# Second norm's rows on VectorE, expert weights split behind the last residual, the second expert's gather asked for later, and two tiles weighed by diagonal matmuls, in a two-layer trunk

## The chip, the cores and the metric

The kernel runs on one core of a Trainium2 chip. The metric is the device time of one execution in microseconds (us). Three runs of the kernel before gave a median of 2047.85 us (2045.67 to 2050.42). About 0.2% of that, 4 us, is what a measurement of this kernel can tell from no change.

Engine names in the rows: PE is TensorE, DVE is VectorE, ACT is ScalarE, POOL is GpSimd, SP is SyncE (here it only issues DMAs).

## What is computed

Two layers over 256 latent tokens and 256 context tokens of width 1024, all in float32. Each layer mixes the tokens (three branches, an output projection and a gated residual), then runs a mixture of 16 experts, of which each token takes two. What the change touches is the second half of a layer and the way into the next one:

```
mix = merge_branches(gate_l, y_hy, y_gdn, y_mla, lp['w_out'])
x = x + (gt1 * mix).astype(x.dtype)
h2 = rms_norm(x, lp['norm2_g']) * (1.0 + sc2) + sh2
x = x + (gt2 * moe_ffn(h2, ...)).astype(x.dtype)
...
# moe_ffn: two experts of 16 per token, with weights that sum to 1
for e in range(N_EXPERTS):
    he = jax.nn.silu(h @ lp['moe_w1'][e]) * (h @ lp['moe_w3'][e])
    out = out + gate[:, e:e + 1] * (he @ lp['moe_w2'][e])
```

The first layer updates all 512 tokens, the second the 256 latent ones alone. A final RMSNorm follows.

## The kernel before

**Tiles.** Tokens lie in tiles of 128 rows, four in layer 0 (two latent, two context), two in layer 1. Buffers are pages of 128x512 floats, taken from a pool; most rows of the trace call them `pg`, and PSUM banks `bank`. One helper (line 207) records every operation, so that rows of the trace tell operations apart by tiles and shapes and not by lines.

**Order.** The order of the instructions on each engine is fixed when the program is built: work is written as items (weights, their preparation, matmuls, what comes behind them) and as streams, which are Python generators with a priority. A planner keeps a modelled clock for each engine and lets a stream go on where the engine that it needs would be idle. Each engine then runs its queue strictly in order.

**Weights in layer 0.** A 128x1024 block of weights is split into a high part (ACT, a CAST to fp32r) and a low part (DVE, a subtraction, `TENSOR_TENSOR pg<-pg,pg 128x1024 fp32r`). `mm3` then makes each product out of three fp32r matmuls. `prep_ahead` (line 520) splits blocks some items ahead of their use; the flag `quiet` holds it still. Layer 1's experts (`moe_sets`) use plain f32 matmuls and split nothing.

**The second norm and the route.** `wout_items` (line 1783) makes the output projection in two groups of two tiles, tile 1 of a group four steps behind tile 0. Behind a tile's last matmul stands its residual on DVE (two pairs of 128x512 operations), and then its stream `ffn_in` (line 1863): squares on ACT, transposes on PE, a Newton chain of twelve small DVE operations for the factor `r` (tiles `t_rf0` to `t_rf3`), the row h2 = (x r) A2 + B2, its DMA to DRAM (`h2d`), and the router's scores. In layer 0 the row is one DVE `TENSOR_SCALAR` and two POOL `TENSOR_TENSOR`s, in layer 1 it goes without A2 and B2. When all scores are there, the stream `route` (line 1930) picks two experts for each token (tiles `t_rsc`, `t_rsel`, `t_rpr`, `t_rgs`, `t_rmx`, `t_rt`, `t_rmk`, `t_rtop`, `t_rix`, `t_rxf`, `t_ro`, `t_rA`), gathers expert 0's rows by a matmul of h2 with a one-hot matrix, and for experts 1 to 3 asks POOL for gathers by index from `h2d` (`t_gi`). `route` does the first three tiles' selection ahead of the last one's. At its gathers it clears `quiet` (line 2047).

**Experts.** An expert of layer 0 (`moe_items`) has two halves j, each with four steps q of six matmuls, and then its second projection; 12 blocks of weights in all. At step (0, 0) of expert e it starts the stream `expert_in` of expert e+1: eight PE transposes of the gathered rows and their split. Layer 1 goes by 12 sets (`moe_sets`) of four experts' quarters, and starts the next set's rows at the same place.

**Between the layers.** The experts' outputs lie in DRAM (`yd`). `load_y` loads both of a tile's outputs, tiles 0 to 3 in order. `combine` (line 2387) weighs each tile's pair (ACT y0 gw0, then DVE y1 gw1 + y0), multiplies by the gate (POOL for three tiles, DVE for the last), adds to the residual (DVE) and squares (ACT). Then a Newton chain for all four tiles, the first norm of layer 1, transposes on PE, and layer 1's input projection. From the last matmul of layer 0's experts until those transposes PE has nothing to do.

## Time and profile before

| | |
|---|---|
| median of three runs | 2047.85 us |
| the profiled execution's own time | 2048.27 us, of which its span is 2045.2 |
| PE busy | 1842.3 us (90%) |
| DVE busy | 1281.2 us (63%) |
| ACT busy | 870.9 us (43%) |
| POOL busy | 312.1 us (15%) |
| layer 0, output projection to first expert | 785 to 885 us of the span |
| layer 0, experts | 885 to 1157 us |
| between the layers | 1157 to 1190 us |
| layer 1, route and first set | 1740 to 1773 us |
| layer 1, experts | to 2034 us |

PE is busy nine tenths of the time; what the kernel could save elsewhere shows only where PE waits. A timeline row gives the start, the duration, the engine, the helper's line, the operation with output and inputs, the count of like operations that were put together, and in brackets how long the engine stood idle before the row and what it waited for.

### The profile page before, as it was taken

Reading aid. Unit: us, or ns where it says so; the run is one execution under the profiler, and the core shown is the slowest. Engines: PE = TensorE matmul, PEld = TensorE weight load, DVE = VectorE, ACT = ScalarE, POOL = GpSimd, SP = SyncE. Lnnn points to the kernel's source line nnn. Section 1 sums busy time; section 2 is a strip of 40 time slices with the busy share of each in tenths; the row PEclk is TensorE's granted clock in tenths of the full one; section 3 lists DMA queues with packets and bytes.
Section 4 is the critical chain, followed back from the end, with each engine's and each line's share of the span. In section 5 each row is a group of like instructions: output and inputs, shape, how many; then the busy total and the mean of one; then the engine's idle time right before and its main releaser. Section 6 shows DMA issues by size and latency. Waiting matters only on the chain. (4 is left out here: it accounts for less than half of the span.)

```text
span 2045.2 us, 32512 instructions
## 1 busy us (share of the span) xinstructions
PE 1842.3 (90%) x12356; PEld 1358.6 (66%) x12357; DVE 1281.2 (63%) x2721; ACT 870.9 (43%) x1518; POOL 312.1 (15%) x323
## 2 busy tenths in 40 slices
PE   4899998999999989699999668998989968799997
PEld 1776786777778777578888546797867966333332
DVE  2667665755675669789999676768668665211113
ACT  3442423444433533278888544343554533111111
POOL 2212112000033104301110112121011211011000
PEclk9999998999999988799999889998989989899999
DMA  9816202602263255689999293822415428899991
GB/s 330 270 60 215 81 19 55 167 21 73 83 206 84 81 207 195 237 306 381 379 382 380 101 335 136 249 60 58 124 32 165 133 96 308 310 314 391 393 390 72
DMA packets 308207, 402.78 MB, mean 197 GB/s; under 512 B 56504, under 2 KB 198334, under 8 KB 308040
## 3 DMA queue, kind: packets, MB, share of 16 engines
q1 hardware_dynamic: 283480, 358.29, 52.6%
q0 software_dynamic: 14112, 30.94, 4.4%
q10 hardware_dynamic: 10448, 11.37, 1.7%
q8 instruction: 99, 1.62, 0.3%
q14 instruction: 68, 0.56, 0.1%
HBM read 391.94 MB, written 24.25 MB: 203 GB/s over the span
## 5 line engine op out<-in xcount | busy, mean ns | idle before, releaser
L207 PE MATMUL bank<-pg,pg 128*128 128x512 f32 (+7 forms) x10694 | 1649.4, 390 | 42.6 <-DVE pg L207 20.0
L207 PEld LDWEIGHTS bank<-pg,pg 128*128 128x128 f32 (+5 forms) x10694 | 1199.5, 166 | 439.9 <-issue 203.8
L207 DVE TENSOR_TENSOR pg<-pg,pg 128x1024 fp32r<-128x1024 f32 (+10 forms) x684 | 598.9, 909 | 156.1 <-ACT pg L207 149.1
L207 ACT CAST pg<-pg 128x1024 fp32r<-128x1024 f32 (+2 forms) x456 | 424.6, 967 | 191.9 <-DVE pg L207 133.2
L207 ACT COPY pg<-bank 64x256 f32<-64x256 f32 (+4 forms) x398 | 162.6, 441 | 282.2 <-PE bank L207 258.8
L207 PE MATMUL bank<-cst,pg 128*128 128x128 f32 (+3 forms) x935 | 149.0, 297 | 121.9 <-DVE pg L207 76.4
L207 PEld LDWEIGHTS bank<-cst,pg 128*128 128x128 f32 (+1 forms) x935 | 122.4, 165 | 169.8 <-issue 55.9
L207 POOL TENSOR_TENSOR pg<-pg,pg 128x512 f32<-128x512 f32 (+3 forms) x65 | 105.8, 1631 | 396.7 <-DVE pg L207 165.7
L207 ACT ACTIVATE pg<-bank 128x512 f32<-128x512 f32 (+1 forms) x116 | 61.2, 535 | 168.3 <-PE bank L207 160.2
L207 ACT ACTIVATE pg<-pg 128x512 f32<-128x512 f32 (+4 forms) x77 | 52.7, 692 | 146.5 <-DVE pg L207 113.5
L207 DVE SCALAR_TENSOR_TENSOR pg<-bank,vec,pg 128x510 f32<-128x510 f32 (+3 forms) x112 | 73.5, 657 | 57.9 <-ACT pg L207 55.9
L207 DVE SCALAR_TENSOR_TENSOR pg<-pg,bank 128x512 f32<-128x512 f32 (+1 forms) x92 | 54.4, 600 | 83.6 <-ACT pg L207 67.5
L207 POOL DMA_INDIRECT yd<-pg,t_vi x26 | 27.1, 1043 | 422.0 <-ACT pg L207 236.7
L207 DVE TENSOR_TENSOR pg<-pg,bank 128x512 f32<-128x512 f32 (+1 forms) x48 | 29.7, 618 | 87.1 <-PE bank L207 78.7
L207 DVE TENSOR_TENSOR pg<-bank,pg 128x512 fp32r<-128x512 f32 (+4 forms) x120 | 69.1, 596 | 22.4 <-ACT pg L207 7.6
L207 ACT CAST pg<-bank 128x512 fp32r<-128x512 f32 (+1 forms) x72 | 35.6, 517 | 102.0 <-PE bank L207 82.5
L207 POOL TENSOR_TENSOR pg<-pg 128x512 f32<-128x512 f32 (+1 forms) x14 | 17.2, 1236 | 401.0 <-ACT pg L207 350.9
L207 ACT ACTIVATE pg<-bank,vec 128x512 f32<-128x512 f32 (+3 forms) x64 | 41.4, 646 | 63.4 <-PE bank L207 58.8
L207 ACT ACTIVATE pg<-bank,t_amx,t_asq 128x512 f32<-128x512 f32 (+1 forms) x48 | 33.9, 707 | 74.9 <-DVE t_amx L207 74.9
L207 PE MATMUL bank<-pg,sc 128*32 128x512 f32 x384 | 54.1, 634 | 0.7 <-DMA pg<-in_w_ada_dram 0.7
L207 DVE COPY pg<-bank 128x512 f32<-128x512 f32 x10 | 6.9, 691 | 69.1 <-PE bank L207 62.2
L207 DVE TENSOR_REDUCE pg<-pg 128x128 f32<-128x1024 f32 (+15 forms) x128 | 43.0, 336 | 4.4
(268 smaller groups left out, 804.7 us busy)
## 6 DMA issues: line engine op xcount, KB each, us to landing
pg<-in_moe_w_dram SPq DMA_DIRECT2D x384, 512.0 KB
pg<-in_w_in_dram SPq DMA_DIRECT2D x120, 512.0 KB
pg<-in_w_ada_dram SPq DMA_DIRECT2D x96, 512.0 KB
pg<-in_w_out_dram SPq DMA_DIRECT2D x24, 512.0 KB
pg<-gcd POOLq DMA_DIRECT2D x16, 256.0 KB, 4.0
pg<-in_hy_out_dram SPq DMA_DIRECT2D x8, 512.0 KB
pg<-in_mla_out_dram SPq DMA_DIRECT2D x8, 512.0 KB
...
```

Of the source, the lines that this page charges most:

```text
L207: return f(*a, **k)
```

## The change

1. **Second norm, layer 0.** The row h2 leaves `ffn_in` and becomes a stream of its own, `row_out`, started behind the score. It is two DVE operations now, (x r) A2 by `SCALAR_TENSOR_TENSOR` and + B2 by `TENSOR_TENSOR`; POOL keeps the DMA. `route` waits for a tile's `row` ahead of the one-hot matmul and of the index part.
2. **Splits.** `quiet` is set from step 8 of the last group of the output projection on, and no longer at the last residual. Of expert 0's blocks one is split ahead of the route now, before it were four.
3. **Gather.** The rows of expert 1 (layer 0) and of set 1 (layer 1) are asked for at step (1, 0) of the first expert or set, so that their transposes stand behind its first half; later ones as before.
4. **Combine.** Tiles 0 and 2 run on ACT and DVE alone. For tiles 1 and 3, `diagonals` makes diagonal matrices of the weights (four 128x128 DVE operations, ahead of the outputs' last scatter), and PE adds up both products in PSUM (eight f32 matmuls 128x512); gate and residual then go in halves of 512 columns. `load_y` loads tiles in the order 0, 2, 1, 3. POOL has no part left.

The core of the diff:

```diff
@@ wout_items
+                if last and k > 7:
+                    self.quiet = True
...
-                    self.quiet = t == tiles - 1
@@ ffn_in
-        if l < L - 1:
-            A2, B2 = self.mod2[i]
-            v.tensor_scalar(h.f(), x.f(), r, None, op0=OP.mult)
-            g_.tensor_tensor(h.f(), h.f(), A2.f(), op=OP.mult)
-            g_.tensor_tensor(h.f(), h.f(), B2.f(), op=OP.add)
...
+        if l < L - 1:
+            self.start(f"row{t}", self.row_out(l, t, x, r), 2)
+
+    def row_out(self, l, t, x, r):
+        v = self.nc.vector
+        A2, B2 = self.mod2[t // 2]
+        h = self.h2[t]
+        yield
+        v.scalar_tensor_tensor(h.f(), x.f(), r, A2.f(), op0=OP.mult, op1=OP.mult)
+        v.tensor_tensor(h.f(), h.f(), B2.f(), op=OP.add)
...
+        self.nc.gpsimd.dma_start(out=self.h2d[l][128 * t:128 * t + 128], in_=h.f())
@@ route
+            for t in range(a, z):
+                yield f"row{t}"
...
+        for t in range(k):
+            yield f"row{t}"
@@ moe_items
-                if j == 0 and q == 0 and e + 1 < NE:
+                if (j, q) == ((0, 0) if e else (1, 0)) and e + 1 < NE:
@@ moe_sets
-                if j == 0 and q == 0 and n + 1 < NSET:
+                if (j, q) == ((0, 0) if n else (1, 0)) and n + 1 < NSET:
@@ load_y
-        for t in range(tiles):
+        for t in (0, 2, 1, 3):
@@ diagonals
+        self.dg = {t: self.M.get() for t in DIAG}
+        for t in DIAG:
+            for i in range(2):
+                self.nc.vector.tensor_scalar(self.dg[t].f(128, 128 * i), self.c("ident"), self.gw[i][:, t:t + 1], None, op0=OP.mult)
@@ combine
+        for t in DIAG:
+            for hf in range(2):
+                b = bank[t, hf] = self.bank()
+                for i in range(2):
+                    nc.tensor.matmul(b, self.dg[t].f(128, 128 * i), ys[t, i].f(512, 512 * hf), start=i == 0, stop=i == 1)
...
+            if t in DIAG:
+                for hf in range(2):
+                    o = 512 * hf
+                    v.tensor_tensor(y0.f(512, o), bank[t, hf], g.f(512, o), op=OP.mult)
...
+                    v.tensor_tensor(x.f(512, o), x.f(512, o), y0.f(512, o), op=OP.add)
+                    nc.scalar.activation(y1.f(512, o), x.f(512, o), AF.Square, accum_out=s8[:, 2 * t + hf:2 * t + hf + 1])
```

**DVE, layer 0, ahead of the last residual.** Tile 2's row (`pg_611`), its score, the first three tiles' selection up to `t_rgs`, then the residual of tile 3, which is the first `SCALAR_TENSOR_TENSOR` from a bank to a 128x512 page. Before:

```order
L207 TENSOR_SCALAR pg_611_6418<-pg_550_6020,t_rf2b 128x1024
L207 TENSOR_TENSOR pg_616_6463<-pg_560_6056,pg_615_6462 128x1024
L207 SCALAR_TENSOR_TENSOR score<-bank_65,t_rf2b,t_cB 128x16
L207 TENSOR_SCALAR t_rsc<-t_rsc 128x48
L207 TENSOR_TENSOR t_rsel<-t_rsc,rb 128x48
L207 TENSOR_TENSOR t_rpr<-t_rsel 128x12x3
L207 TENSOR_TENSOR t_rpr<-t_rsel 128x12x2
L207 TENSOR_TENSOR t_rpr<-t_rsel 128x12
L207 TENSOR_REDUCE t_rgs<-t_rpr 128x12
L207 TENSOR_TENSOR pg_620_6485<-pg_563_6074,pg_619_6484 128x1024
L207 TENSOR_TENSOR pg_624_6499<-pg_574_6132,pg_623_6498 128x1024
L207 SCALAR_TENSOR_TENSOR pg_627_6512<-bank_63,pg_553_6026 128x512
```

Now:

```order
L207 TENSOR_REDUCE t_rgs<-t_rpr 128x12
L207 SCALAR_TENSOR_TENSOR pg_611_6416<-pg_550_6020,t_rf2b,pg_557_6036 128x1024
L207 TENSOR_TENSOR pg_611_6416<-pg_611_6416,pg_558_6038 128x1024
L207 TENSOR_REDUCE t_rmx<-t_rgs 128x3
L207 TENSOR_TENSOR t_rt_6208<-t_rgs,t_rmx 128x12
L207 TENSOR_TENSOR t_rt_6208<-t_rt_6208,cst_72 128x12
L207 TENSOR_REDUCE t_rmx<-t_rt_6208 128x3
L207 TENSOR_TENSOR t_rgm<-t_rt_6208,t_rmx 128x12
L207 SCALAR_TENSOR_TENSOR pg_624_6508<-bank_63,pg_553_6026 128x512
L207 TENSOR_TENSOR pg_551_6022<-pg_551_6022,pg_624_6508 128x512
L207 SCALAR_TENSOR_TENSOR pg_624_6508<-bank_66,pg_553_6026 128x512
L207 TENSOR_TENSOR pg_551_6022<-pg_551_6022,pg_624_6508 128x512
```

The splits of blocks 560, 563 and 574 are gone from this place; tile 2's row (two operations) and five small ones stand there.

**PE, layer 0, expert 0.** The end of step (0, 0) and the transposes of expert 1's gathered rows (`cst<-` is the identity). Before:

```order
L207 MATMUL bank_66<-pg_608_6407,pg_636_6674 128x512
L207 MATMUL bank_66<-pg_607_6406,pg_637_6675 128x512
L207 MATMUL bank_69<-cst_71,pg_629_6518 128x128 x4
L207 MATMUL bank_68<-cst_71,pg_629_6518 128x128 x4
L207 MATMUL bank_66<-pg_615_6462,pg_636_6674 128x512
L207 MATMUL bank_66<-pg_616_6463,pg_636_6674 128x512
```

Now, at the end of step (1, 0):

```order
L207 MATMUL bank_69<-pg_647_6741,pg_633_6664 128x512
L207 MATMUL bank_69<-pg_646_6740,pg_634_6665 128x512
L207 MATMUL bank_68<-cst_71,pg_626_6514 128x128 x4
L207 MATMUL bank_70<-cst_71,pg_626_6514 128x128 x4
L207 MATMUL bank_69<-pg_648_6744,pg_633_6664 128x512
L207 MATMUL bank_69<-pg_649_6745,pg_633_6664 128x512
```

Four steps more, 24 matmuls, stand ahead of the transposes. On DVE, ten splits stand between the last `t_gw` and the first of expert 0's results where seven stood, and the rows' split stands behind the seventh, where it stood ahead of all; from expert 2 on, the kinds of operation come in the same order in both.

**DVE, between the layers.** `combine` from tile 0's residual on; `bank` is now an input. Before:

```order
L207 TENSOR_TENSOR pg_548_6016<-pg_548_6016,pg_1332_9823 128x1024
L207 SCALAR_TENSOR_TENSOR pg_1336_9831<-pg_1337_9833,t_gw,pg_1336_9831 128x1024
L207 TENSOR_TENSOR pg_549_6018<-pg_549_6018,pg_1334_9827 128x1024
L207 SCALAR_TENSOR_TENSOR pg_1338_9835<-pg_1339_9837,t_gw,pg_1338_9835 128x1024
L207 TENSOR_TENSOR pg_1338_9835<-pg_1338_9835,pg_632_6525 128x1024
L207 TENSOR_TENSOR pg_550_6020<-pg_550_6020,pg_1336_9831 128x1024
L207 TENSOR_TENSOR pg_551_6022<-pg_551_6022,pg_1338_9835 128x1024
L207 TENSOR_SCALAR t_css<-t_css 128x4
```

Now:

```order
L207 TENSOR_TENSOR pg_548_6016<-pg_548_6016,pg_1333_9824 128x1024
L207 SCALAR_TENSOR_TENSOR pg_1335_9828<-pg_1336_9830,t_gw,pg_1335_9828 128x1024
L207 TENSOR_TENSOR pg_1335_9828<-pg_1335_9828,pg_629_6521 128x1024
L207 TENSOR_TENSOR pg_550_6020<-pg_550_6020,pg_1335_9828 128x1024
L207 TENSOR_TENSOR pg_1337_9832<-bank_67,pg_628_6519 128x512
L207 TENSOR_TENSOR pg_549_6018<-pg_549_6018,pg_1337_9832 128x512
L207 TENSOR_TENSOR pg_1337_9832<-bank_70,pg_628_6519 128x512
L207 TENSOR_TENSOR pg_549_6018<-pg_549_6018,pg_1337_9832 128x512
L207 TENSOR_TENSOR pg_1339_9836<-bank_68,pg_629_6521 128x512
L207 TENSOR_TENSOR pg_551_6022<-pg_551_6022,pg_1339_9836 128x512
L207 TENSOR_TENSOR pg_1339_9836<-bank_69,pg_629_6521 128x512
L207 TENSOR_TENSOR pg_551_6022<-pg_551_6022,pg_1339_9836 128x512
```

Tile 2's residual moved ahead of tile 1's, and the last two tiles' work is in halves that wait for PE.

## Rows read from the trace of the kernel before

**Rows 1.** Windows: bounds, us, busy by engine, PEclk, DMA share, GB/s:

```profile
900.00:950.00 50.00, 50.00 (x235) 41.13 (x234) 47.30 (x48) 43.35 (x54) 7.11 (x6) 1.00 1.01 381
1190.00:1195.00 5.00, 4.40 (x19) 3.90 (x20) 1.97 (x5) 3.34 (x5) 0.00 (x0) 0.50 1.13 326
1800.00:1950.00 150.00, 150.00 (x1368) 48.60 (x1364) 23.23 (x51) 20.80 (x44) 15.68 (x19) 1.00 1.04 377
```

**Rows 2.** PE's timeline, last projection to first expert; columns start, us, row, [idle before]:

```profile
840.83 1.12 PE L207 MATMUL bank<-cst,pg 128*128 128x128 f32 x4 [7.99 <-DVE pg L207]
...
851.65 0.20 PE L207 MATMUL bank<-t_rA,t_uSb 128*128 128x48 bf16 x1 [5.16 <-DVE t_rA L207]
...
852.55 8.14 PE L207 MATMUL bank<-pg,pg 128*128 128x128 f32 x48 [0.67 <-DVE pg L207]
...
871.60 1.97 PE L207 MATMUL bank<-cst,pg 128*128 128x128 f32 x8 [6.07 <-DMA pg<-h2d,t_gi]
873.22 12.12 PE L207 MATMUL bank<-pg,pg 128*128 128x512 f32 x48
```

**Rows 3.** Timelines between the layers, DVE, then ACT, then PE:

```profile
1168.75 1.28 DVE L207 SCALAR_TENSOR_TENSOR pg<-pg,t_gw,pg 128x1024 f32<-128x1024 f32 x1 [14.53 <-ACT pg L207]
...
1174.86 3.20 DVE L207 SCALAR_TENSOR_TENSOR pg<-pg,t_gw,pg 128x1024 f32<-128x1024 f32 x1
1182.51 3.50 DVE L207 TENSOR_TENSOR pg<-pg,pg 128x1024 f32<-128x1024 f32 x3
...
1173.51 1.15 ACT L207 ACTIVATE pg<-pg,t_gw 128x1024 f32<-128x1024 f32 x1 [1.28 <-DMA pg<-yd]
...
1190.30 1.04 PE L207 MATMUL bank<-cst,pg 128*128 128x128 f32 x3 [33.52 <-DVE pg L207]
```

**Rows 4.** PE's timeline, layer 1, first set:

```profile
1748.99 1.92 PE L207 MATMUL bank<-pg,pg 128*32 128x512 f32 x16
1757.65 1.97 PE L207 MATMUL bank<-cst,pg 128*128 128x128 f32 x8 [6.74 <-DMA pg<-h2d,t_gi]
1759.55 5.90 PE L207 MATMUL bank<-pg,pg 128*32 128x512 f32 x40
```

**Rows 5.** DVE's timeline, last projection to the route:

```profile
830.08 0.75 DVE L207 TENSOR_SCALAR pg<-pg,t_rf2b 128x1024 f32<-128x1024 f32 x1
...
834.52 2.40 DVE L207 TENSOR_TENSOR t_rpr<-t_rsel 128x36 f32<-128x36 f32 x3
...
837.10 2.35 DVE L207 TENSOR_TENSOR pg<-pg,pg 128x1024 fp32r<-128x1024 f32 x2
839.37 0.68 DVE L207 SCALAR_TENSOR_TENSOR pg<-bank,pg 128x512 f32<-128x512 f32 x1
...
848.88 2.47 DVE L207 TENSOR_TENSOR t_ro<-cst,t_rxf 128x48 f32<-128x48 f32 x2
...
853.13 0.33 DVE L207 TENSOR_TENSOR t_rpr<-t_rsel 128x12 f32<-128x12 f32 x3
...
855.58 0.26 DVE L207 TENSOR_TENSOR t_ro<-cst,t_rxf 128x16 f32<-128x16 f32 x2
```

**Rows 6.** POOL's timeline, the rows of tiles 2 and 3:

```profile
830.98 5.70 POOL L207 TENSOR_TENSOR pg<-pg,pg 128x1024 f32<-128x1024 f32 x2 [10.89 <-DVE pg L207]
...
837.56 2.75 POOL L207 MEMSET pg<- 128x1024 f32 x3
846.49 4.80 POOL L207 TENSOR_TENSOR pg<-pg,pg 128x1024 f32<-128x1024 f32 x2 [6.18 <-issue]
```

**Rows 7.** DVE's timeline behind the route, at the gather's landing:

```profile
873.43 1.49 DVE L207 TENSOR_TENSOR pg<-bank,pg 128x512 fp32r<-128x512 f32 x2 [6.35 <-issue]
875.17 8.11 DVE L207 TENSOR_TENSOR pg<-pg,pg 128x1024 fp32r<-128x1024 f32 x7 [0.25 <-ACT pg L207]
883.20 0.68 DVE L207 SCALAR_TENSOR_TENSOR pg<-pg,bank 128x512 f32<-128x512 f32 x1
```

**Rows 8.** PE's timeline, the f32 matmuls 128x512 at the kernel's end:

```profile
2027.13 7.12 PE L207 MATMUL bank<-pg,pg 128*128 128x512 f32 x16 [0.48 <-PEq L2577]
```

More of the change, by code (lines that the diff above doesn't have):

```diff
@@ L1881, in ffn_in @@
         self.rsqrt(r, ss[:, 0:1], tmp)
-        if l < L - 1:
-            A2, B2 = self.mod2[i]
-            v.tensor_scalar(h.f(), x.f(), r, None, op0=OP.mult)
-            g_.tensor_tensor(h.f(), h.f(), A2.f(), op=OP.mult)
-            g_.tensor_tensor(h.f(), h.f(), B2.f(), op=OP.add)
-            if t % 2 == 1:
-                A2.free()
-                B2.free()
-        else:
+        if l == L - 1:
             nc.scalar.activation(h.f(512), x.f(512), AF.Copy, scale=r)
             v.tensor_scalar(h.f(512, 512), x.f(512, 512), r, None, op0=OP.mult)
-        g_.dma_start(out=self.h2d[l][128 * t:128 * t + 128], in_=h.f())
+            g_.dma_start(out=self.h2d[l][128 * t:128 * t + 128], in_=h.f())
         self.h2[t] = h
@@ L2385, in load_y, with diagonals, combine @@
         return ys
-    def combine(self, tiles, ys, parts, after):
+    def diagonals(self):
+        self.dg = {t: self.M.get() for t in DIAG}
+        for t in DIAG:
+            for i in range(2):
+                self.nc.vector.tensor_scalar(self.dg[t].f(128, 128 * i), self.c("ident"), self.gw[i][:, t:t + 1], None, op0=OP.mult)
+    def combine(self, ys, after):
         nc, M = self.nc, self.M
         v = nc.vector
-        n = D // parts
-        units = [(t, n * i) for t in tiles for i in range(parts)]
-        ss = self.tiny(8, "css")
-        def weigh(u, t, o):
-            y0, y1 = ys[t, 0].f(n, o), ys[t, 1].f(n, o)
-            nc.scalar.activation(y0, y0, AF.Copy, scale=self.gw[0][:, t:t + 1])
-            v.scalar_tensor_tensor(y0, y1, self.gw[1][:, t:t + 1], y0, op0=OP.mult, op1=OP.add)
-        def gate(u, t, o):
-            y0 = ys[t, 0].f(n, o)
-            (v if u == len(units) - 1 else nc.gpsimd).tensor_tensor(y0, y0, self.gt2[t // 2].f(n, o), op=OP.mult)
-        def add(u, t, o):
-            x = self.xt[t].f(n, o)
-            v.tensor_tensor(x, x, ys[t, 0].f(n, o), op=OP.add)
-        def square(u, t, o):
-            x = self.xt[t].f(n, o)
-            nc.scalar.activation(ys[t, 1].f(n, o), x, AF.Square, accum_out=ss[:, u:u + 1])
-            if o + n == D:
-                ys[t, 0].free()
-                ys[t, 1].free()
-                self.dump(f"xout{t}", self.xt[t].f())
-                after(t)
-        for s in range(len(units) + 2):
-            for k, f in ((0, weigh), (0, gate), (1, add), (2, square)):
-                if 0 <= s - k < len(units):
-                    f(s - k, *units[s - k])
-        return ss[:, :len(units)]
@@ new lines, in combine @@
+        ss, s8 = self.tiny(4, "css"), self.tiny(8, "css8")
+        bank = {}
+        for t in DIAG:
[3 more added lines that the diff above has]
+                    nc.tensor.matmul(b, self.dg[t].f(128, 128 * i), ys[t, i].f(512, 512 * hf), start=i == 0, stop=i == 1)
+            self.dg[t].free()
+        plain = [t for t in range(4) if t not in DIAG]
+        for t in plain:
+            nc.scalar.activation(ys[t, 0].f(), ys[t, 0].f(), AF.Copy, scale=self.gw[0][:, t:t + 1])
@@ new lines, in combine @@
+        for t in (*plain, *DIAG):
+            g, x = self.gt2[t // 2], self.xt[t]
+            y0, y1 = ys[t, 0], ys[t, 1]
+            if t in DIAG:
+                for hf in range(2):
+                    o = 512 * hf
+                    v.tensor_tensor(y0.f(512, o), bank[t, hf], g.f(512, o), op=OP.mult)
+                    self.unbank(bank[t, hf])
+                    v.tensor_tensor(x.f(512, o), x.f(512, o), y0.f(512, o), op=OP.add)
+                    nc.scalar.activation(y1.f(512, o), x.f(512, o), AF.Square, accum_out=s8[:, 2 * t + hf:2 * t + hf + 1])
+            else:
+                v.scalar_tensor_tensor(y0.f(), y1.f(), self.gw[1][:, t:t + 1], y0.f(), op0=OP.mult, op1=OP.add)
+                v.tensor_tensor(y0.f(), y0.f(), g.f(), op=OP.mult)
+                v.tensor_tensor(x.f(), x.f(), y0.f(), op=OP.add)
+                nc.scalar.activation(y1.f(), x.f(), AF.Square, accum_out=ss[:, t:t + 1])
+            y0.free()
+            y1.free()
+            after(t)
@@ L2423, in layer @@
+        for t in DIAG:
+            v.tensor_tensor(ss[:, t:t + 1], s8[:, 2 * t:2 * t + 1], s8[:, 2 * t + 1:2 * t + 2], op=OP.add)
+        return ss
     def layer(self, l):
@@ L2529, in build @@
             self.drain(("filters",) if l < L - 1 else ("partial",))
+            if l < L - 1:
+                self.diagonals()
             self.overflow(l)
```

8 lines of the change are left out of this document (6 added, 2 removed).

## The prediction

> **What bounds the kernel now.** I read the windows first, since a share of busy time over the whole span hides the stages. In the experts of layer 0 PE is busy 50.00 of 50.00 us at full clock, and so it is in the experts of layer 1, 150.00 of 150.00 [rows 1]. What these stages cost is PE's own work, which the change leaves alone. It can gain only where PE waits, and PE's timeline shows where. In layer 0 it waits 7.99 us for the residual of tile 3, 5.16 for the route's choice (`t_rA`) and 6.07 for expert 1's gathered rows [rows 2]; between the layers 33.52 us for the first norm of layer 1 [rows 3]; in layer 1 6.74 us for set 1's rows [rows 4]. All parts of the change are aimed at one of these five waits. So the sum is: how much earlier does PE's next work start, at each.
>
> **Layer 0, the residual of tile 3.** DVE's queue runs in order, and the residual starts at 839.37 [rows 5]. Since 830.08 there stand ahead of it the operation for tile 2's row (0.75), a split alone and two more (2.35 the two, so 1.18 each), and the selection of three tiles. The change takes away 0.75 + 3 x 1.18 = 4.3 us. The selection is also slow: three `t_rpr` operations take 2.40 there, and 0.33 at 853.13 on a third of the columns [rows 5]. The slow ones lie under POOL's pair from 830.98 for 5.70 us [rows 6]; at 853.13 POOL runs no such pair. I take POOL's pair as the cause. That is 2.1 us on `t_rpr`, and I estimate some 1.6 for the other slow one, `t_rsc`, which stands between the two rows 830.08 and 834.52. POOL's pair goes: 3.7 us less. Put in ahead of the residual are tile 2's row, 1.28 for its first operation [rows 3] and 1.18 for its second [rows 5], 2.5 together, and five small operations, about 1.0. Net 839.37 - 4.3 - 3.7 + 2.5 + 1.0 = 834.9; the split that goes also covered most of the wait for ACT's scores, which I put at 0.6. So the residual starts at about 835.5, **3.9 us** earlier. There is a floor: PE's projection ends where its idle time begins, 840.83 - 7.99 = 832.84 [rows 2], so that no more than 6.5 can come.
>
> **Layer 0, from residual to the one-hot matmul.** Before, PE's matmul of rows and one-hot starts at 852.55 [rows 2], 13.2 us behind the residual's start. In that stretch POOL's pair from 846.49 [rows 6] lies over the cast of the indices and over two `t_ro` operations, 2.47 against 0.26 at 855.58 [rows 5]. With the cast, which I put at 1.4 lost, it is 3.6 us. The 0.75 operation goes as well. Tile 3's row comes, 2.5 us, and in DVE's queue it stands ahead of the one-hot, so all of it is on the path. Parts of the selection move into the wait for PE's scores, which I estimate at 0.6. Net 3.6 + 0.75 + 0.6 - 2.5 = **2.4 us**. The price of a new wait is in this: `route` waits for tile 3's row, and behind it on DVE are the one-hot and all splits.
>
> **Layer 0, the gather.** Before, DVE stands idle for 6.35 us until the gathered rows are there, since their split is next in its queue, and then does seven splits (8.11, so 1.16 each) until expert 0's first result at 883.20 [rows 7]. After, three splits more must be done before that result, and the idle time is there for them. From the start of the idle time, 873.43 - 6.35 = 867.08: ten splits 11.6 and the rows 1.49 end at 880.2, and the result starts 3.0 us earlier, counted from a route that ends when it did. PE has to be ready by then: behind the fourth split it needs six matmuls and eight transposes (1.97 at most), which is done well before. PE's 6.07 us [rows 2] are thus the upper bound, nothing the lower (if PE, paced by a split each 1.16 us, falls to half clock); I take **3.0**. What is late next is DVE with the splits, not the gather.
>
> So layer 0 gives 3.9 + 2.4 + 3.0 = 9.3 us. All of it is carried through the experts only if nothing else sets their pace. DVE is busy 47.30 of 50 us there [rows 1], so it has 5% to spare, and the order is the same from expert 2 on, with each split as far ahead of its use as it was. The 3 splits that the change takes from ahead of the route are in the sum above.
>
> **Between the layers.** Four steps in a row set the end before: DVE weighs and POOL gates, and DVE's work beside POOL's pair is stretched, 3.20 where 1.28 is alone [rows 3]. Then three DVE operations of 3.50 together from 1182.51, then ACT's squares, the chain, the norm. After, tiles 0 and 2 take DVE 2 x (1.28 + 2 x 1.18) = 7.3 us from 1168.75, so to about 1176.2 with the wait for tile 2's load. The load that ACT waits for at 1173.51 [rows 3] is the fifth, and tile 1 takes that place; PE starts there. A diagonal matmul takes 7.12 / 8 = 0.89 at full clock (two records each [rows 8]); at half clock twice that, 1.78. PE comes from a long wait and starts at half clock, as it does before behind this wait: 0.50 over 5 us of work [rows 1], the time of three such matmuls. With two to four of the eight at half clock the last ends between 1182.4 and 1184.2; I take 1183. Behind it come gate and residual of the last half, 0.69 each by the half-size operation [rows 5], and what stood behind the last residual before: from 1182.51 + 3.50 = 1186.0 to PE's transposes at 1190.30 it is 4.3 [rows 3]; half a square less and two small sums more leave that as it is. So PE starts at 1183 + 1.4 + 4.3 = 1188.7, **1.5 us** earlier. Bounds: all eight at half clock end at 1187.7 and cost 3.1 us instead; two at half clock, and a clock that is up for a part of layer 1's first transposes, give 2.5. The four diagonals are 128x128 on DVE while it has 14.53 us idle [rows 3], and cost nothing. The loads' order costs nothing either: tile 2 is worked on second.
>
> **Layer 1, the first set.** No split stands there, so PE can run steps (0, 1) to (0, 3) and (1, 0) in the 6.74 us that it waits [rows 4]. Their pace is 40 records in 5.90, so 16 records in 2.36 with half clock at the start, and 1.92 in the first step [rows 4]. Three steps are 48 records and 5.1 to 7 us, so the wait is nearly filled. From 4.0 to 6.7; I take **5.5**. PE is busy all through the sets [rows 1], so it is carried to the end.
>
> Sum: 9.3 + 1.5 + 5.5 = 16.3 us. The profiled execution took 2048.27 us, 0.4 above the median, so 2048.3 - 16.3 = **2032.0 us**. Forecast, from 2028 to 2036: chance 0.48.
>
> **Rivals.**
>
> 1. *The clock stays up.* PE's wait for tile 3 falls from 8 us to 4, and the half-clock work behind it (840.83 and 852.55, 8.14 for 48 records [rows 2]) could run at full clock. For that: both stretches are cheaper by some 2 us each at full clock, and 2 more between the layers. Against: waits of 3 us and more remain. 2032 - 6 = 2026. Chance 0.14.
> 2. *The diagonals are slow.* All eight at half clock, 4.7 us worse than my sum: 2036.7. For it: the half clock at 1190 [rows 1]. Against: eight matmuls in a row are work without a gap. Chance 0.13.
> 3. *The row pair is stretched.* It has two SBUF operands in both operations and stands on the path twice, where POOL still runs a MEMSET (2.75 us at 837.56 [rows 6]) and DMA issues. Beside POOL's pair an operation of 1.28 took 3.20 [rows 3]; a pair so stretched costs about 4.1 more, two of them 8.2, and the route would gain nothing: 2032 + 8.2 = 2040. Against: the two splits from 837.10 lie beside that MEMSET and take 1.18 each [rows 5]. Chance 0.10. [...]
> 4. *The shift is not carried.* The DMA share is 1.01 and 1.04 in the experts [rows 1]. If weights rather than PE set the pace, layer 0's or layer 1's gain is taken back by a wait for weights: 2032 + 9.3 = 2041, 2032 + 5.5 = 2037.5, or both, 2046.8. Against: PE waits nowhere in those windows. Chance 0.10.
> 5. *DVE becomes the bound of layer 0's experts (slower).* It has 2.7 us in 50 to spare, so 1.0 per expert of some 18 (272 us from 885 to 1157 for 15 of them). If the lost lead of three splits means that PE waits for a split in each expert, and each of 15 experts takes 1.1 us longer, the gain of 16.3 is gone; from there on the kernel is slower. At 1.25 us each: 2032 + 18.8 = 2050.8. Against: the order is the same there. Chance 0.03.
> 6. *The change doesn't do what it says.* DVE is not stretched by POOL but by something that stays: then 3.7 + 3.6 are missing, 2032 + 7.3 = 2039. Chance 0.02.
>
> **How the numbers follow.** 0.2% of the time, 4 us, is about what a measurement can tell from no change. Faster by more than that is below 2043.8, which holds in all cases but the fifth and some ends of the fourth, where both gains are lost: 0.92. Within 0.2%: 0.05. Slower: 0.03. The range leaves out 2 in 10: the lower half of the first rival and the outer end of the forecast's unknown sizes below, and the ends of the fourth, the fifth and parts of the third above: 2024 to 2041.
>
> **What would show it.** In the profile after: the wait of PE for the residual about 4 us and not 8; no wait for `h2d` rows in either layer; DVE's small operations at 0.2 to 0.3 us throughout the route; PE's wait between the layers split in two, before the diagonals and behind them; PE still 50.00 of 50.00 in the experts. The prediction is wrong if DVE's row operations take far over 1.3 us, if PE waits for DVE in the experts, or if the last diagonal matmul ends behind 1186 by before's times.

## The result and the profile after

The changed kernel takes 2022.13 us (median of four runs, 2019.62 to 2026.38), beside four runs of the kernel before at 2046.76: a ratio of 0.9876, 95% interval 0.9859 to 0.9893. It gains 24.6 us where 16.3 were forecast; 2022.13 lies below the range. Of the 9.9 us by which it lies below 2032.0, 8.3 are gain; 1.5 are the base, since the sum starts from a profiled run of 2048.27 and the kernel before measured 2046.76 beside the changed one.

The page of the profile after, span and first part (busy us by engine):

```profile
span 2017.9 us, 32558 instructions
PE 1846.1 (91%) x12372; PEld 1359.6 (67%) x12373; DVE 1271.1 (63%) x2736; ACT 869.6 (43%) x1520; POOL 288.2 (14%) x312
```

PE's timeline after, layer 0, answering to [rows 2]:

```profile
831.96 0.72 PE L207 MATMUL bank<-cst,pg 128*128 128x128 f32 x4 [3.69 <-DVE pg L207]
...
837.47 0.20 PE L207 MATMUL bank<-t_rA,t_uSb 128*128 128x48 bf16 x1
...
840.80 8.12 PE L207 MATMUL bank<-pg,pg 128*128 128x128 f32 x48 [3.09 <-DVE pg L207]
...
856.49 7.08 PE L207 MATMUL bank<-pg,pg 128*128 128x512 f32 x23 [2.50 <-DVE pg L207]
863.40 1.03 PE L207 MATMUL bank<-cst,pg 128*128 128x128 f32 x8
```

The wait for the residual is 3.69 us where it was 7.99. The wait for `t_rA` is gone, but one of 3.09 for tile 3's row and the one-hot stands behind it. At expert 1's transposes (863.40) there is no bracket: the gather is hidden. In its place PE waits 2.50 us for a split, at 856.49.

PE between the layers, answering to [rows 3], and in layer 1's first set, answering to [rows 4]:

```profile
1157.15 8.56 PE L207 MATMUL bank<-pg,pg 128*128 128x512 f32 x16 [16.11 <-DMA pg<-yd]
1171.20 1.14 PE L207 MATMUL bank<-cst,pg 128*128 128x128 f32 x3 [5.49 <-DVE pg L207]
...
1729.48 8.79 PE L207 MATMUL bank<-pg,pg 128*32 128x512 f32 x80
1738.94 1.09 PE L207 MATMUL bank<-cst,pg 128*128 128x128 f32 x8 [0.67 <-DMA pg<-h2d,t_gi]
```

The one wait of 33.52 us is cut in two by the diagonals (8.56 us). In layer 1 80 records stand ahead of set 1's transposes where 16 stood, and the wait is 0.67 where it was 6.74.

DVE after, answering to [rows 5] and [rows 7]:

```profile
826.13 0.19 DVE L207 TENSOR_SCALAR t_rsc<-t_rsc 128x48 f32<-128x48 f32 x1 [0.31 <-ACT t_rsc L207]
...
826.59 0.38 DVE L207 TENSOR_TENSOR t_rpr<-t_rsel 128x36 f32<-128x36 f32 x3
...
827.15 1.27 DVE L207 SCALAR_TENSOR_TENSOR pg<-pg,t_rf2b,pg 128x1024 f32<-128x1024 f32 x1
828.46 1.22 DVE L207 TENSOR_TENSOR pg<-pg,pg 128x1024 f32<-128x1024 f32 x1
...
830.50 0.68 DVE L207 SCALAR_TENSOR_TENSOR pg<-bank,pg 128x512 f32<-128x512 f32 x1
...
855.22 8.03 DVE L207 TENSOR_TENSOR pg<-pg,pg 128x1024 fp32r<-128x1024 f32 x7
864.66 1.29 DVE L207 TENSOR_TENSOR pg<-bank,pg 128x512 fp32r<-128x512 f32 x2 [1.41 <-ACT pg L207]
```

The selection's operations are short (`t_rpr` 0.38 where it was 2.40), the row takes 1.27 and 1.22, the residual of tile 3 starts at 830.50, and the 6.35 us of idle time ahead of the rows' split are 1.41.

**Stage by stage.** The table below is worked out from PE's timelines: an instruction that stands in both traces marks the stage's start and its end, "busy" is the time inside PE's records between them, "idle" the rest.

| stage, by times of before | before: busy + idle | after: busy + idle | change | forecast |
|---|---|---|---|---|
| first group's last transposes to tile 3's (798.33 to 840.83) | 33.84 + 8.66 | 30.70 + 4.36 | -7.44 | -3.9 |
| to the one-hot matmul (852.55) | 5.69 + 6.03 | 5.15 + 3.69 | -2.88 | -2.4 |
| to 1000, the gather in it | 140.82 + 6.76 | 140.56 + 3.16 | -3.86 | -3.0 |
| 1140 to layer 1's transposes (1190.30) | 16.39 + 33.52 | 24.90 + 21.60 | -3.41 | -1.5 |
| layer 1, 1746 to 1900 | 145.99 + 8.14 | 143.76 + 2.08 | -8.30 | -5.5 |
| sum | | | -25.9 | -16.3 |

Outside these stages the two traces differ by 0.9 us in sum up to PE's last instruction (1.4 gained ahead of 785, which the change doesn't touch, 0.5 lost in all other places). The two profiled runs lie 28.7 us apart, 4 more than the medians, because that of before is slower than its median and that of the changed kernel faster; so the sum of the stages is only roughly the gain. The stages themselves repeat: the trace of the changed kernel's second measurement (`r_after` below) has each of the five within 0.1 us. Two things stand out. The waits shrank by nearly what was forecast: 4.30, 2.34, 3.60 and 6.06 against 3.9, 2.4, 3.0 and 5.5. And PE's own work became cheaper, by 3.14 us in the first stage and 2.23 in layer 1, although its instructions there are the same. The sum of the forecast has no term for that.

### The profile page after: what moved, and what is told of

Its sections match the earlier page's. It is cut to its first block, busy times and chain, and to the rows that moved or that the text cites. A ratio compares the mean times of both kernels' runs of the same rounds, so it can differ in the third digit from the quotient of the medians.

```text
span 2017.9 us, 32558 instructions
## 1 busy us (share of the span) xinstructions
PE 1846.1 (91%) x12372; PEld 1359.6 (67%) x12373; DVE 1271.1 (63%) x2736; ACT 869.6 (43%) x1520; POOL 288.2 (14%) x312
## 5 line engine op out<-in xcount | busy, mean ns | idle before, releaser
L207 DVE TENSOR_TENSOR pg<-pg,pg 128x1024 fp32r<-128x1024 f32 (+13 forms) x691 | 600.7, 902 | 157.7 <-ACT pg L207 151.9
L207 POOL TENSOR_TENSOR pg<-pg,pg 128x256 f32<-128x256 f32 (+3 forms) x54 | 76.2, 1415 | 370.4 <-ACT pg L207 175.8
```

Of the source, the lines that this page charges most:

```text
L207: return f(*a, **k)
```

## The experiments

The theory to test: part of the gain is PE's own work, which ran at half clock (a granted clock of 0.50, as at 1190 us in [rows 1]) around the waits and now runs at full clock (the expectations call it C). Its rivals: only the waits were mis-sized, and each part is worth what it takes off a wait (W); or the splits and the combine are worth far more than forecast.

| kernel | median us | ratio to before, 95% |
|---|---|---|
| the changed kernel again (`r_after`) | 2022.22 | 0.9885 (0.9871 to 0.9899) |
| changed, row on POOL (`u1_row_pool`) | 2027.67 | 0.9912 (0.9899 to 0.9925) |
| changed, `quiet` as before (`u2_splits`) | 2022.33 | 0.9880 (0.9864 to 0.9896) |
| changed, layer 0's gather as before (`u3a_gather0`) | 2024.25 | 0.9890 (0.9871 to 0.9910) |
| changed, layer 1's gather as before (`u3b_gather1`) | 2031.39 | 0.9932 (0.9915 to 0.9949) |
| changed, combine as before (`u4_combine`) | 2021.52 | 0.9880 (0.9866 to 0.9895) |
| before, with part 3 alone (`b_gather`) | 2030.56 | 0.9917 (0.9900 to 0.9934) |
| before, with part 1 alone (`b_row`) | 2038.91 | 0.9955 (0.9939 to 0.9971) |
| parts 1 and 3 (`p13`) | 2022.47 | 0.9875 (0.9855 to 0.9895) |
| before, PE kept busy in layer 1's wait (`b_warm_l1`) | 2043.84 | 0.9985 (0.9973 to 0.9997) |
| before, PE kept busy at 800 us (`b_warm_l0`) | 2047.88 | 1.0005 (0.9993 to 1.0016) |
| changed, kept busy around the diagonals (`a_warm_comb`) | 2018.51 | 0.9859 (0.9845 to 0.9873) |
| changed, kept busy at five places (`a_warm_all`) | 2018.63 | 0.9862 (0.9843 to 0.9882) |
| parts 1 and 3, kept busy between the layers (`p13_warm`) | 2021.60 | 0.9871 (0.9849 to 0.9892) |
| changed, five places, one moved (`a_warm_v2`) | 2015.47 | 0.9849 (0.9827 to 0.9870) |

**Each part undone.** First the changed kernel once more, beside the five.

> The changed kernel once more, beside the runs below, as their reference. Both theories: about 2022 us, 24.6 us below the kernel before. Theory W (the prediction's own way of counting): the change is worth the waits of PE that it takes away, 16 us, and the rest was chance of the runs; then new runs fall back towards 2031. Theory C: a wait of PE costs, besides its length, time at half clock behind it, and that came back too; then the new runs stay at 2022 and the profile shows fewer stretches at 0.50 in the first norm of layer 0's second half (around 806 us), behind the gathers and behind the diagonals.

It came out as it had. Part 1 undone: the row back in `ffn_in` on POOL, no `row_out`.

```diff
+            v.tensor_scalar(h.f(), x.f(), r, None, op0=OP.mult)
+            g_.tensor_tensor(h.f(), h.f(), A2.f(), op=OP.mult)
+            g_.tensor_tensor(h.f(), h.f(), B2.f(), op=OP.add)
...
-        if l < L - 1:
-            self.start(f"row{t}", self.row_out(l, t, x, r), 2)
```

> The changed kernel with the second norm's row made by one VectorE operation and POOL's pair again. Theory W: 3.8 us slower (POOL's stretching returns with 7.3, two VectorE pairs of 2.5 go, two operations of 0.75 return): 2026. Theory C: the row's own stream also changed how PE's work around 806 us is mixed, and with it the clock there; 3.8 plus about 3.4, 2029; the profile shows PEclk 0.50 from about 806 to 813 us again.

It is 5.5 us slower than the changed kernel. Its DVE and POOL timelines, tile 2:

```profile
828.51 2.11 DVE L207 TENSOR_SCALAR t_rsc<-t_rsc 128x48 f32<-128x48 f32 x1 [0.31 <-ACT t_rsc L207]
...
830.90 2.40 DVE L207 TENSOR_TENSOR t_rpr<-t_rsel 128x36 f32<-128x36 f32 x3
...
828.20 4.86 POOL L207 TENSOR_TENSOR pg<-pg,pg 128x1024 f32<-128x1024 f32 x2 [9.42 <-DVE score L207]
```

With POOL's pair back, from 828.20 to 833.06, two operations under it are long again (2.11 and 2.40 for 0.19 and 0.38); `t_rsel` between them is not (0.21). POOL's pair is the cause, as the prediction took it. The first of the two, `t_rsc`, has a single input tile.

Part 2 undone:

```diff
-                if last and k > 7:
-                    self.quiet = True
...
+                    self.quiet = t == tiles - 1
```

> The changed kernel, but the splits are held still only behind the last residual, as before: three more splits ahead of the route. Theory W: 3.5 us of VectorE ahead of the residual return, up to 1.2 come back at the gather, where the three splits are then done: 2 to 4 us slower, 2024 to 2026. Theory C: the same, and PE's longer wait for the residual lets no more clock go than now, since it falls there in either kernel (0.50 from 832 to 846 us): no difference between the theories here.

It is 0.1 us slower than the changed kernel; the expected 2 to 4 are not there. Its PE timeline shows why, at the first expert:

```profile
853.47 7.22 PE L207 MATMUL bank<-pg,pg 128*128 128x512 f32 x30
861.97 1.09 PE L207 MATMUL bank<-cst,pg 128*128 128x128 f32 x8 [1.28 <-DMA pg<-h2d,t_gi]
```

With the splits done early PE runs all 30 records of the first steps without the 2.50 us wait for a split that the changed kernel has behind 7 of them. The stage up to 1000 is 6.5 us shorter than before there, against 3.9 in the changed kernel; the two stages ahead of it lose 2.2 (the wait of the first is 2.5 longer, and PE's busy time there happens to be 1.4 shorter). What the splits gain ahead of the route they give back at expert 0.

Part 3 undone, in layer 0 and in layer 1:

```diff
-                if (j, q) == ((0, 0) if e else (1, 0)) and e + 1 < NE:
+                if j == 0 and q == 0 and e + 1 < NE:
```

> The changed kernel, but in layer 0 expert 1's rows are asked for at step (0, 0) again. The prediction's sum: 3.0 us slower than the changed kernel (2025.2), as DVE stands idle at the gather again; by the stretch from the one-hot matmul into the experts, in which the changed kernel is 3.9 us shorter than before. If the gains of the parts hang together (the splits held back are paid for in DVE's idle time at the gather, which this kernel fills no more, since the rows' split stands ahead of them again): 3.9 plus the 3.5 of three splits, 6 to 8 us slower (2028 to 2030).

```diff
-                if (j, q) == ((0, 0) if n else (1, 0)) and n + 1 < NSET:
+                if j == 0 and q == 0 and n + 1 < NSET:
```

> The changed kernel, but in layer 1 set 1's rows are asked for at step (0, 0) again, as before. Theory W: slower than the changed kernel by the wait that returns, 5.5 us or so (2027.6). Theory C: by the wait and by the half clock behind it, 8 us (2030); in the profile the eight transposes take 1.97 us again where the changed kernel took 1.09, and PEclk reads 0.50 for some microseconds behind the wait.

Layer 0's is worth 2.0 us here (2.4 in the trace, in the stage up to 1000), less than expected; layer 1's is worth 9.2. Layer 1's is the largest single term, and larger than the wait that it removes. Its PE timeline:

```profile
1740.32 1.97 PE L207 MATMUL bank<-cst,pg 128*128 128x128 f32 x8 [6.78 <-DMA pg<-h2d,t_gi]
1742.22 15.33 PE L207 MATMUL bank<-pg,pg 128*32 128x512 f32 x128
```

The wait is back with 6.78 us. The eight transposes take 1.97 where the changed kernel has 1.09 (1738.94 above).

Part 4 undone: `diagonals` out, `combine` and `load_y` as before.

```diff
-        for t in (0, 2, 1, 3):
+        for t in range(tiles):
...
-                    b = bank[t, hf] = self.bank()
...
+            (v if u == len(units) - 1 else nc.gpsimd).tensor_tensor(y0, y0, self.gt2[t // 2].f(n, o), op=OP.mult)
```

> The changed kernel with the combine between the layers as before (POOL gates, no diagonals, loads in the order 0 to 3). Theory W: 1.5 us slower than the changed kernel (2023.6). Theory C: 3.5 us slower (2025.6), since PE's diagonals bring the clock up in mid-course and the last ones run at full clock; the difference is at PE's first transposes of layer 1.

In its trace the stage up to 1190.30 is 0.3 us shorter than before, against 3.4 in the changed kernel, so the diagonals bring 3.1 there. The median is 0.7 us lower than the changed kernel's, within the intervals. A gain at the place is shown; one in the total is not.

**Parts alone, on the kernel before.** `b_gather` has the two lines of part 3, `b_row` part 1's `row_out` with its waits, `p13` is the changed kernel with parts 2 and 4 undone as above.

```diff
-                if j == 0 and q == 0 and e + 1 < NE:
+                if (j, q) == ((0, 0) if e else (1, 0)) and e + 1 < NE:
...
-                if j == 0 and q == 0 and n + 1 < NSET:
+                if (j, q) == ((0, 0) if n else (1, 0)) and n + 1 < NSET:
```

> The kernel before with the third part alone: rows of expert 1 and of set 1 asked for at step (1, 0), in both layers. If the parts add up: 8.3 us in layer 1 (6.1 of PE's wait, 2.2 of its own work that ran at half clock) and 3 to 4 in layer 0, 11 to 13 us faster than the kernel before, 2034. If layer 0's share needs the other parts: 8 to 9 us faster, 2037.5.

```diff
+            self.start(f"row{t}", self.row_out(l, t, x, r), 2)
...
+            for t in range(a, z):
+                yield f"row{t}"
```

> The kernel before with the first part alone: the row as a stream of its own, by two VectorE operations. By the prediction's steps 3.8 us faster (7.3 of stretching go, two pairs of 2.5 come, two operations of 0.75 go): 2042.7. If the parts add up with the later gather's 16 us: 5.5 to 8 us faster, 2038.5 to 2041. If the stretch at half clock around 806 us hangs on the order of this row's work, the profile shows no 0.50 from 806 to 813 us and the stretch from the last group's projection to the residual of tile 3 loses 1.5 to 3 us of PE's own time.

```diff
-                if last and k > 7:
-                    self.quiet = True
...
-                self.diagonals()
```

> The changed kernel without its second and fourth part: the row by VectorE and the later gather alone, splits and combine as before. Undone one at a time, the splits cost +0.1 us and the combine -0.7. If they are worth nothing: 2022, as the changed kernel. If each hides the other's loss or gain: 2025 or more.

Part 3 alone brings 16 us, part 1 alone 8, both together 24: the gain of the changed kernel. The rival by which the splits and the combine are worth far more than forecast falls. PE's timeline of `b_gather` shows part 3 at both places:

```profile
860.67 7.16 PE L207 MATMUL bank<-pg,pg 128*128 128x512 f32 x30
868.04 1.09 PE L207 MATMUL bank<-cst,pg 128*128 128x128 f32 x8 [0.21 <-DMA pg<-h2d,t_gi]
...
1738.81 8.78 PE L207 MATMUL bank<-pg,pg 128*32 128x512 f32 x80
1748.27 1.09 PE L207 MATMUL bank<-cst,pg 128*128 128x128 f32 x8 [0.69 <-DMA pg<-h2d,t_gi]
```

In layer 0 the wait is 0.21 where it was 6.07, and the stage up to 1000 is 7.6 us shorter. Part 3 is worth more here than in the changed kernel, since four splits are done ahead.

`b_row` shortens the first stage by 5.1 us, and 3.13 of that is PE's busy time: 30.71, as in the changed kernel (30.70). The kernels that keep the row on POOL have 33.84, 32.36, 32.48 and 33.84 (before, `u1_row_pool`, `b_gather`, `b_warm_l1`), the ten that have it as a stream and nothing added in this stage 29.32 to 30.72. So the two groups don't overlap, but 1.4 us of such a difference comes and goes within either. The windows of before, and under them of the changed kernel, at the place (columns as in [rows 1]):

```profile
806.70:813.50 6.80, 6.80 (x21) 5.64 (x21) 6.45 (x13) 0.63 (x1) 5.20 (x4) 0.50 0.77 258
```

```profile
806.70:813.50 6.80, 6.80 (x36) 5.72 (x35) 6.59 (x12) 0.00 (x0) 0.59 (x1) 1.00 0.97 314
```

PE is busy all 6.80 us in both, at half clock before (0.50, 21 records), at full clock after (1.00, 36). What PE did ahead of the fall, before and then after:

```profile
804.00 4.39 PE L207 MATMUL bank<-t_rwA,pg 128*128 128x16 f32 x32
```

```profile
802.57 1.86 PE L207 MATMUL bank<-t_rwA,pg 128*128 128x16 f32 x16
804.27 1.64 PE L207 MATMUL bank<-pg,pg 128*128 128x512 f32 x6
805.75 1.85 PE L207 MATMUL bank<-t_rwA,pg 128*128 128x16 f32 x16
```

Before, 32 router matmuls of 16 columns stand in a row; with the row as a stream, six matmuls of 512 columns stand between two lots of 16. Three more traces give the granted clock in the same two windows, 803.50 to 806.70 and 806.70 to 813.50: with 32 in a row 0.50 and 0.75 (`b_gather`) and 0.87 and 0.81 (`u1_row_pool`), with the six between 0.52 and 1.00 (`b_row`); before has 1.00 and 0.50, the changed kernel 1.00 and 1.00. From 806.70 on these windows go with the order; ahead of it `b_row` and `b_gather` have a low clock in either order. That this order is what keeps the clock up was not tested apart from the rest of part 1.

**The price of a wait.** The half clock is tested where nothing else moves: in the kernel before, five f32 matmuls of constants fill most of layer 1's wait, and the wait's end stays. `warm(n)` issues n such matmuls into a free bank that nothing reads.

```diff
+    def warm(self, n):
+        b = self.bank()
+        self.plan.off = True
+        for i in range(n):
+            self.nc.tensor.matmul(b, self.c("ident"), self.cst[1][:, :512], start=i == 0, stop=i == n - 1)
+        self.plan.off = False
+        self.banks.appendleft(b)
@@ expert_in
+        if l == L - 1 and e == 1:
+            self.warm(5)
```

> The kernel before with five f32 matmuls 128x512 of constants, into a bank that nobody reads, put on PE ahead of the transposes of set 1's rows in layer 1: they fill 5 to 6 of the 6.74 us that PE waits there, and the wait itself stays (the gather lands when it did). Theory W: no gain, 0 to 1 us slower. Theory C: 2 to 2.5 us faster than the kernel before, since the transposes (1.97) and the first matmuls behind them run at full clock; PEclk 1.00 from the transposes on.

PE's timeline, and the windows behind the wait, of before and of `b_warm_l1`:

```profile
1750.77 4.56 PE L207 MATMUL bank<-cst,cst 128*128 128x512 f32 x10
1757.51 1.09 PE L207 MATMUL bank<-cst,pg 128*128 128x128 f32 x8 [2.18 <-DMA pg<-h2d,t_gi]
1758.53 13.94 PE L207 MATMUL bank<-pg,pg 128*32 128x512 f32 x128
```

```profile
1757.70:1762.40 4.70, 4.70 (x24) 2.31 (x28) 1.36 (x4) 1.50 (x4) 0.99 (x1) 0.50 0.82 294
```

```profile
1757.55:1762.25 4.70, 4.70 (x44) 2.01 (x48) 1.37 (x4) 1.50 (x4) 0.99 (x1) 1.00 0.56 196
```

The gather lands when it did (1757.65 and 1757.51), but the work behind it runs at a granted clock of 1.00 and not 0.50: 44 records in 4.70 us and not 24. The stage is 2.3 us shorter, the median 2.5, with an interval that leaves out 1. PE's busy time in the stage, less the 4.56 added, is 143.64, as in the changed kernel (143.76). So of the 8.3 us that part 3 gained there, 6.1 were the wait and 2.2 the half-clock work behind it: the theory holds at this place.

The same, at the end of layer 0's first group:

```diff
@@ ffn_in, behind the transposes
+        if l == 0 and t == 1:
+            self.warm(3)
```

> The kernel before with three such matmuls behind tile 1's transposes in layer 0, in PE's wait of 2.4 us at 801.6. Theory W: no gain, up to 1 us slower. Theory C: the stretch at 0.50 from 806.69 to 813.52 goes, the projection of the last group ends 3 us earlier and, since tile 2's residual waits for it, so does all behind it: about 3 us faster.

No gain, where 3 us were expected. PE's own work in the stage is cheaper, although the 32 router matmuls still stand in a row. But PE has no wait there to fill: its busy time in the stage is 32.16 us, of which the added three take 2.67. Without them it would be 29.5, 4.3 less than before; since 1.4 of that comes and goes by itself, the half clock at the router's matmuls cost some 3 by this estimate. On the busy engine the added matmuls cost most of what they bring, 2.67 of these 3 us.

**The waits that are left.** The last group keeps PE busy in the changed kernel's own waits: 16 matmuls ahead of the diagonals, 5 behind them; then also 4 in layer 1's route, 3 in the wait for tile 3's residual and 3 ahead of the last one-hot.

```diff
@@ combine
+        self.warm(16)
         bank = {}
...
+        self.warm(5)
         plain = [t for t in range(4) if t not in DIAG]
```

> The changed kernel with 16 such matmuls on PE ahead of the diagonals (14.3 us at full clock, in a wait of 16.1) and five between the diagonals and the first transposes of layer 1 (4.5 us in a wait of 5.5). Theory W: no gain, or a loss where they delay the diagonals. Theory C: the diagonals take 7.1 us where they took 8.56, the first 32 transposes about 3.5 where they took 6.7, so 3 to 4 us faster than the changed kernel, 2018 to 2019.

```diff
@@ wout_items
+                    if l == 0 and t == tiles - 1:
+                        self.warm(3)
@@ route
+                if l == L - 1:
+                    self.warm(4)
...
+            if a > 0:
+                self.warm(3)
```

> The changed kernel with constants' matmuls in five of PE's waits: 16 ahead of the diagonals and five behind them, three ahead of the residual's transposes of tile 3 in layer 0 (wait of 3.7 us), three ahead of its last one-hot (3.1), four ahead of layer 1's route (4.3). Theory C: on top of the 3.7 us of the two places between the layers, the router's scores and one-hot of layer 0 (3.43 and 8.12 us now) take about 1.9 and 5.5 and layer 1's one-hot (6.38) about 4: 4 to 7 us more, 2012 to 2015. Theory W: 2018.5 as with the two places, or slower by what the added matmuls delay.

3.7 and 3.6 us below the changed kernel in the medians, the second far from what was expected. The first looks as expected, but its trace doesn't bear it out. PE behind the diagonals, the changed kernel and then `a_warm_comb`:

```profile
1172.63 5.57 PE L207 MATMUL bank<-cst,pg 128*128 128x128 f32 x29 [0.30 <-ACT pg L207]
...
1179.70 0.98 PE L207 MATMUL bank<-pg,pg 128*128 128x512 f32 x3 [1.25 <-DVE pg L207]
```

```profile
1172.70 3.38 PE L207 MATMUL bank<-cst,pg 128*128 128x128 f32 x29 [0.44 <-ACT pg L207]
...
1179.62 7.04 PE L207 MATMUL bank<-pg,pg 128*128 128x512 f32 x15 [3.30 <-DVE pg L207]
```

The transposes are 2.2 us cheaper (in the changed kernel the granted clock over them is 0.59), and PE waits 2.1 longer for DVE behind them. The stage up to layer 1's transposes is 1.0 us shorter than in the changed kernel, the next 59 us 0.2. With an interval that overlaps that of `r_after`, the rest of the 3.7 is not shown to come from these places. `a_warm_all` shows a misplaced edit in layer 0:

```profile
841.34 6.96 PE L207 MATMUL bank<-pg,pg 128*128 128x128 f32 x48 [2.75 <-DVE pg L207]
...
848.24 2.82 PE L207 MATMUL bank<-cst,cst 128*128 128x512 f32 x6
850.89 1.95 PE L207 MATMUL bank<-pg,pg 128*128 128x128 f32 x16
```

The three stand behind the big one-hot, where PE doesn't wait, and add 2.82 us to the path; the 2.75 ahead of it are left idle. Then the transposes without diagonals, on `p13`:

```diff
+                self.warm(36)
                 ss = self.combine(range(4), ys, 1, keep)
```

> Parts one and three alone, without diagonals, but with 36 f32 matmuls of constants on PE in its wait between the layers (32 us of 33 to 34). Theory C: layer 1's transposes and first matmuls run at full clock, 2 to 3 us faster than parts one and three alone (2022.5), 2019 to 2020, so that the diagonals' gain is to be had without them. Theory W: 2022.5, or slower if the added matmuls delay the transposes.

0.9 us below `p13`, within the intervals. PE's timelines, `p13` and then `p13_warm`:

```profile
1177.16 5.12 PE L207 MATMUL bank<-cst,pg 128*128 128x128 f32 x29 [0.29 <-ACT pg L207]
...
1184.28 0.96 PE L207 MATMUL bank<-pg,pg 128*128 128x512 f32 x3 [1.76 <-DVE pg L207]
```

```profile
1177.22 3.39 PE L207 MATMUL bank<-cst,pg 128*128 128x128 f32 x29 [0.44 <-ACT pg L207]
...
1184.20 0.97 PE L207 MATMUL bank<-pg,pg 128*128 128x512 f32 x3 [3.35 <-DVE pg L207]
```

The transposes take 1.7 us less (3.39 for 5.12), and PE then waits 1.6 longer for DVE: its next work starts at 1184.20 where it started at 1184.28. Here the slower transposes cost nothing, since the path goes through DVE; `a_warm_comb` says the same. Last, the five places with the three ahead of the first one-hot:

```diff
-            if a > 0:
+            if l == 0 and a == 0:
                 self.warm(3)
```

> As the changed kernel with matmuls of constants in five waits, but in layer 0 three stand ahead of the first one-hot matmul (wait of 3.1 us) where they stood ahead of the last, small one and cost 2.7 us on the path. Theory C: 2 to 3 us faster than that kernel (2018.6), 2015.5 to 2016.5; the first one-hot matmul takes 5.5 to 6 us where it takes 8.12 in the changed kernel.

```profile
836.25 4.19 PE L207 MATMUL bank<-cst,cst 128*128 128x512 f32 x6
840.27 5.52 PE L207 MATMUL bank<-pg,pg 128*128 128x128 f32 x48
```

The 48 records of the one-hot take 5.52 us where the changed kernel needs 8.12 at a mean granted clock of 0.68, and start no later (840.27 against 840.80). From tile 3's transposes up to 1000 the trace is 3.4 us shorter than the changed kernel's. At 2015.47 us this is the fastest kernel here, 6.7 below the changed one; its interval (0.9827 to 0.9870) just doesn't meet that of `r_after` (0.9871 to 0.9899), and overlaps that of the changed kernel's first four runs (0.9859 to 0.9893). Its mean granted clock over the whole span is 0.966, the changed kernel's 0.955 and 0.952 in its two traces, that of before 0.947; as time at 0.50 instead of 1.00 that is 138 us, 182 and 192, and 218.

## Why the prediction was too small

**What bounds the kernel now.** The step that failed is in this part: "What these stages cost is PE's own work, which the change leaves alone. It can gain only where PE waits". That holds for the experts' stages, and was taken for all others too, so the sum put the work around the waits at nothing. PE's own work has two prices (behind layer 1's wait 24 records in 4.70 us at a granted clock of 0.50 and 44 at 1.00), and the change moved some of it from one to the other: 3.14, 0.54, 0.26 and 2.23 us in the four stages of layers 0 and 1, 6.2 together. `b_warm_l1` shows it for layer 1 by experiment. For the 3.1, `b_row` shows that part 1 alone brings them, give or take the 1.4 that comes and goes. In the first stage it was not even behind a wait of the sum: the half-clock stretch at 806.70 lies some 26 us ahead of the wait that the prediction priced.

**Rival 1, "the clock stays up"**, is what came, priced at 6 and measured at 6.2 in those four stages, though not where it was priced: of its 4 us at the transposes and the one-hot some 0.5 came (the one-hot takes 8.12 us after and 8.14 before), and 3.14 and 2.23 came ahead of them and in layer 1. It was held to be a case of its own with a chance of 0.14; in these traces it is a term of the sum. That its price of 6 came so close is luck, since other places paid it: the wait for the residual shrank by 4.3 us, and the one-hot behind it took as long as before.

**Layer 0, the residual of tile 3.** 3.9 forecast, 4.30 measured in PE's waits. The residual starts at 830.50 where it was 839.37, 8.9 earlier; 1.4 of that comes from ahead of 785, and the 7.4 left are the waits' 4.3 and the 3.1 by which PE's projection itself ends sooner. POOL's pair as the cause is right (`u1_row_pool`).

**From residual to the one-hot matmul.** 2.4 forecast, 2.88 measured, of which 2.34 in waits. The new wait for tile 3's row is there (3.09 at 840.80), as priced.

**The gather.** 3.0 forecast, 3.86 measured, and the reason given holds: DVE's splits are late next (2.50 at 856.49). What that paragraph missed is that part 2 is what makes them late. "The 3 splits that the change takes from ahead of the route are in the sum above" counts them right, but `u2_splits` shows that the exchange is worth nothing either way.

**Between the layers.** 1.5 forecast, 3.41 in the trace: the diagonals took 8.56 us, against some 9.5 in the working, and start 0.7 earlier. Rival 2 is wrong. (By the working's own numbers PE starts 1.6 earlier and not 1.5.) The term was mis-sized by 1.9 in the trace. That this gain reaches the end is not shown: `u4_combine` and `p13` go without it and measure the same.

**Layer 1, the first set.** 5.5 forecast, 6.06 in waits and 8.30 with the clock, 9.2 in the medians. The working counts three steps and 48 records as filling the wait; the steps that it names are four, and the 80 records ahead of the transposes, where 16 stood, are 64 more, 6.9 us of work; so nearly all of the wait went.

**The other rivals.** The row pair takes 1.27 and 1.22 us and is not stretched (3; by its own ratio a stretched pair would cost 3.7 more and not 4.1). PE's time between 1000 and 1140 differs by 0.1 us and from 1300 to 1700 by 0.1, so the shift is carried (4) and DVE is no bound (5). POOL was the cause (6).

So the 9.6 us by which the five stages beat the forecast are 6.2 of clock, 1.5 of waits in layers 0 and 1, and 1.9 between the layers. The medians show 8.3, and by them the gain between the layers may be nothing.

What stays open: whether parts 2 and 4 bring anything in the total (0.1 and -0.7 us, with intervals of 3 us to each side), and what lets the clock fall at 806.70.

## What to carry to other kernels

A wait of PE is priced with the work behind it. Add to the idle time what the next stretch takes at its granted clock over what the same instructions take at full clock: here 2.2 us in layer 1 and 2.6 at the one-hot (8.12 and 5.52). That was an upper bound, which came in layer 1, where the wait went almost wholly (6.74 to 0.67), and not at the one-hot, where 3.09 us of waiting stayed. Look for stretches at half clock where PE is busy, too, as from 806.70 to 813.50 (0.50, PE busy 6.80 of 6.80). Matmuls of constants in a wait that can't be removed bought that part back in two places (2.3 us in `b_warm_l1`, 2.6 at the one-hot of `a_warm_v2`), and only where PE really stood idle and the path went through PE behind the wait: `b_warm_l0` and `p13_warm` gained nothing beyond their intervals. When one part of a change takes splits from one place to another, look at who waits at the other place before counting a gain.

## What the runs showed of the chip beyond that

In `u3b_gather1` the granted clock also falls where PE hardly waits, to a mean of 0.62 under work from 1262 us on, in which PE is busy without a gap and which no part of the change touches; ahead of it PE waits 0.73 us and does eight matmuls of 8 columns, as in the changed kernel. PE's timeline and window there, and then the same of the changed kernel:

```profile
1262.39 8.88 PE L207 MATMUL bank<-pg,pg 128*128 128x128 f32 x48
1262.00:1271.00 9.00, 9.00 (x53) 9.00 (x52) 5.63 (x30) 1.00 (x3) 0.00 (x0) 0.62 1.04 383
```

```profile
1261.86 5.75 PE L207 MATMUL bank<-pg,pg 128*128 128x128 f32 x48
1261.50:1268.00 6.50, 6.50 (x59) 6.05 (x60) 3.86 (x26) 0.26 (x2) 0.00 (x0) 1.00 1.05 382
```

The same 48 records take 8.88 us at a mean clock of 0.62 and 5.75 at 1.00. Of the 17 traces seven have 8.88 to 8.92 us for these 48 records, one (`p13`) has 7.30, and the others have 5.75 to 5.79. What decides it stays open. By such a fall alone this stretch of a single trace is 3.1 us off, which is why the stages above are told by their busy and idle time, and what a kernel gains in all by its median.
